# A hybrid encoder block on one core: the last projection with tokens on the output rows

## The chip, the core and the metric
The kernel runs on one core of one Trainium2 chip. Its time is the device time of one execution, in microseconds (us). The engines are PE (TensorE, matrix products into PSUM), DVE (VectorE), ACT (ScalarE), POOL (GpSimd) and SP (SyncE, which here issues most DMAs). They run beside each other, each in the order in which its instructions were written down, and wait for each other by semaphores.

## What is computed
One encoder layer on 512 tokens of width 2048, in float32: a projection into two recurrent mixers (gated DeltaNet and RWKV-7), an output projection, cross attention into 256 memory tokens, an MLP and a final norm.

```python
xn = _rmsnorm(h, norm_mix[l])
y = xn @ w_in[l]
...
h = h + mixed @ w_out[l]
h = h + _cross_attention(_rmsnorm(h, norm_xattn[l]), _rmsnorm(mem, norm_mem[l]), ...)
hn = _rmsnorm(h, norm_mlp[l])
h = h + jnp.square(jax.nn.relu(hn @ mlp_w_up[l])) @ mlp_w_down[l]
return _rmsnorm(h, norm_final)
```
`mlp_w_up` is 2048 x 8192 and `mlp_w_down` 8192 x 2048. "Up" and "down" below are these two products.

## The kernel before
The residual stands with features on partitions: `hres` is 16 tiles of 128 features x 512 tokens, and `hp` are the same tiles as 8 pairs. Weights are the stationary operand, and tokens move.

Precision: each float32 operand is cut into two float32r parts, `hi` (a cast on ACT) and `lo` (the rest, a subtraction on DVE). A product is hi·hi + hi·lo + lo·hi, three matmuls.

Order: up and down, like the mixers, are written as generators ("chains", lines 1737 to 2115). A list scheduler, `run`, takes at each step the instruction that can start first by its own table of costs (`cost`, `start`), where a chain's rank delays it by 150 ns a step, so the order on each engine, SP's queue among them, is fixed when the program is built. The first part of the program (mixers, key projection `kp`, key-query product `kq`) is one such schedule, and up with down another.

Up: 32 units `("u", p, 0)`, each a 2x2 block product by seven products instead of eight (Strassen-Winograd: B11, B21, B22, T1 to T4). The weight sums s1 to s4 that these need are made by DVE in `adds`; `splits` cuts the weights; `multiply_` issues 8 steps per product, one matmul of 512 columns (hi and lo of 256 token columns side by side) and one of 256. `upout` collects, `squared_` applies the squared ReLU and stores the result to DRAM (`Ud`), and `differences` makes the block sums of half of the units and stores them too (`Xd`).

Down, `units` from line 1730 on, by groups of 1024 hidden rows:
- Groups 0 to 6 have four units each, one for each 512 output columns. The first unit (in group 0 the first two) is plain, `"p"`: four weight tiles of 128 output features, 8 steps of three matmuls with all 512 tokens moving. The others are `"d"`: seven products with 256 columns moving, 24 matmuls each, their weight sums made by `adds` as in up.
- Group 7 is a loop of its own behind the scheduler (line 2176): 32 half tiles of plain products, and in between it the sums of squares of the final norm, by a matmul with ones.
- `plainadd` and `downout` add the banks to `hres` and `hp`; `norm_` has multiplied these by the root of the MLP's norm before, one pair in every fourth up unit.
- `abloads`, `direct_` and `crossed` bring the activations back from DRAM and cut them; group e's blocks are freed by its last unit.
- Buffers: 6 raw weight tiles of 128 x 1024 (`wfree`), 3 cut ones (`hfree`), 8 PSUM banks under five tags.

The end: the second half's sum of squares, a square root and a reciprocal on two columns, a matmul that spreads the result over rows, 16 multiplications and 16 stores.

Of the kernel before, what the change touches and what calls it, by code (L numbers as in the profile page):

```python
# [17 lines left out]
P = 128  # L18
# [55 lines left out]
def build(tc, I, out):  # L74
# [106 lines left out]

    def where(a):
        n = a.tensor.name
        k = slot.get(n, n)
        assert holder.get(k, n) == n, (n, holder[k])
        return k
# [92 lines left out]
    def run():  # L279


        while chains:
            best = None
            for c in list(chains):
# [19 lines left out]
                key = (t + (0 if c[3][0][0] == "PE" else 150 * c[1]), c[1])  # L304
# [71 lines left out]
    kpo = [(0, 0), (1, 0), (0, 1), (1, 1)] + [(n, h) for n in range(2, KD) for h in range(2)]  # L376
    hk = [("w", I["wk"][n][:, h * 1024:(h + 1) * 1024]) for n, h in kpo]
# [151 lines left out]
    def projections():  # L529
# [509 lines left out]
    def gdn(h):  # L1039
# [99 lines left out]
        yield from inverse_levels(f"gi{h}", Tm, Tt, N3, ("gkn", "gk", "gqn"), TtG)  # L1139
        vns, Ss = tl("gE"), tl("gEG")  # L1140
# [74 lines left out]

    issue(pieceload(0))
# [8 lines left out]
    for k in range(6, XA):  # L1225
        issue(xload(k))
    chain(pieces(), 1)
# [455 lines left out]
    Ud = [pd.tile([P, 2, 512], F32, name=f"ud{i}", tag=f"ud{i}") for i in range(32)]  # L1683
    pu_cm = tc.tile_pool(name="pu", bufs=1, reuse_waits="tile")
    pu = pu_cm.__enter__()
    Xd = [pd.tile([P, 1024], F32, name=f"xd{i}", tag=f"xd{i}") for i in range(28)]
    uhl = [], []
# [11 lines left out]
    SV = Lane(nc.scalar, "ACT")  # L1699

# [4 lines left out]
    sfree, abfree = buffers(2, "ws"), buffers(2, "ab")  # L1705
# [29 lines left out]
    A11, A21, A22, A12 = range(4)  # L1735

    def loads():
        for u in units:
            kind, e, g = u
            if kind == "p":  # L1740
                todo = [(n, I["w_dn"][e, g * 4 + n]) for n in range(4)]
            else:
                src = I["w_up"][e] if kind == "u" else I["w_dm"][e, g]
                todo = [(i, src[i]) for i in ((A11, A12, A22, A21) if u == units[0] else (A11, A21, A22, A12))]
            for i, src in todo:
                raws[u, i] = r = yield from take(wfree)
                yield SY.dma_start(r, src)
                events.add(("raw", u, i))
        yield lambda: ("raw", units[-1], A12) in events
        r = yield from take(wfree)  # L1750
        raws["last"] = r
        yield SY.dma_start(r, I["w_dn"][7, 0])
        events.add(("raw", "last"))
# [19 lines left out]
    def adds():  # L1773
        for u in units:
            if u[0] == "p":
                continue
# [23 lines left out]
    def splits():  # L1800
        for u in units:
            if u[0] == "p":
                for n in range(4):
                    yield after("raw", u, n)
                    halves[u, n] = hl = yield from take(hfree)
                    yield from cut(raws[u, n], *hl)
                    wfree.append(raws[u, n])
                    events.add(("cut", u, n))
                continue
# [14 lines left out]
        yield after("raw", "last")  # L1824
        yield lambda: any(x is lastpair[0] for x in hfree)
        hfree[:] = [x for x in hfree if x is not lastpair[0]]
        yield from cut(raws["last"], *lastpair[0])

    lastpair = [hfree[-1]]

# [3 lines left out]
    def multiply_():  # L1834
        for u in units:
            kind, e, g = u
            if kind == "p":
                yield lambda: all(("dir", e, k) in events for k in range(4))
                for n in range(4):
                    pt, key = yield from bank("mm", f"dn{e}_{g}_{n}")  # L1840
                    yield after("cut", u, n)
                    hi, lo = halves[u, n]
                    for k in range(8):
                        sl = slice(k * P, k * P + P)
                        uh, ul = direct[e, k]
                        yield mmr(pt, hi[:, sl], uh, k == 0)
                        yield mmr(pt, hi[:, sl], ul)
                        yield mmr(pt, lo[:, sl], uh, stop=k == 7)
                    hfree.append(halves[u, n])
                    chain(plainadd(e, 4 * g + n, pt, key), 1)  # L1850
                continue
            first = u == units[0]
            for i, w in order_of(u):
# [9 lines left out]
                if kind == "u":  # L1863
                    for zs in (range(7), range(7, 8)) if first else (range(8),):
                        for k in zs:
                            yield mmr(pt, hi[:, k * P:k * P + P], comb[i][k], fresh and k == 0)
                        for k in zs:
                            yield mmr(pt[:, HA], lo[:, k * P:k * P + P], comb[i][k][:, HA], stop=k == 7)
                    if e == 31:
                        tfree.extend(comb[i])  # L1870
                else:
                    yield lambda: all(i in blocks.get((e, k), ()) for k in range(4))
                    for q in range(2):
                        o = pt[:, q * M:q * M + M]
                        for k in range(4):
# [451 lines left out]
```

## Time and profile before
| | us |
|---|---|
| three runs, median (lowest to highest) | 2946.62 (2946.21 to 2946.89) |
| the profiled execution, its own time | 2946.95 |
| its span | 2945.2 |

A profile comes from one execution. Its page gives the busy time of each engine, the span in 40 slices, the chain of work that ended last, and groups of equal instructions. A group's line names the source line, the engine, the operation and output<-inputs; then come busy time, mean ns of one, and the idle time before it with what ended that. Most instructions of the scheduled parts have line L251, where the scheduler issues them, so groups are told apart by tile names: `py` is the input projection, `kq` the key-query product, `mxu`, `mmu` and `mgu` are up's banks, `dn` a plain unit's, `mxd`, `mmd` and `mgd` those of the seven-product units. Matmuls are pipelined, so the distance from one start to the next tells more than a duration. In a timeline the first number is the start, the second the length.

### The profile page before, as it was taken

Reading aid. Unit: us, or ns where it says so; the run is one execution under the profiler, and the core shown is the slowest. Engines: PE = TensorE matmul, PEld = TensorE weight load, DVE = VectorE, ACT = ScalarE, POOL = GpSimd, SP = SyncE. Lnnn points to the kernel's source line nnn. Section 1 sums busy time; section 2 is a strip of 40 time slices with the busy share of each in tenths; the row PEclk is TensorE's granted clock in tenths of the full one; section 3 lists DMA queues with packets and bytes.
Section 4 is the critical chain, followed back from the end, with each engine's and each line's share of the span. In section 5 each row is a group of like instructions: output and inputs, shape, how many; then the busy total and the mean of one; then the engine's idle time right before and its main releaser. Section 6 shows DMA issues by size and latency. Waiting matters only on the chain.

```text
span 2945.2 us, 51704 instructions
## 1 busy us (share of the span) xinstructions
PE 2920.6 (99%) x20570; PEld 2527.8 (86%) x20570; DVE 2317.8 (79%) x3535; ACT 1552.3 (53%) x2227; POOL 213.9 (7%) x552
## 2 busy tenths in 40 slices
PE   9999999999999999999999999999999999999998
PEld 7877787887778888889988888888888999999997
DVE  7677676676778767679848998989898888888877
ACT  7455555555556655654436555555555444444434
POOL 0212302302223000000000000000000000000000
PEclk9999999999999999999999999999999999999999
DMA  5323332332425487774323344444445534444435
GB/s 188 113 86 86 98 97 82 98 97 82 132 75 174 167 281 250 253 239 135 109 86 101 136 150 148 146 147 154 144 158 186 186 141 147 150 166 150 143 113 181
DMA packets 228451, 425.22 MB, mean 144 GB/s; under 512 B 92073, under 2 KB 115885, under 8 KB 228209
## 3 DMA queue, kind: packets, MB, share of 16 engines
q1 hardware_dynamic: 211216, 388.35, 40.3%
q10 hardware_dynamic: 16992, 33.56, 3.0%
q8 instruction: 162, 2.65, 0.4%
q14 instruction: 81, 0.66, 0.1%
HBM read 366.91 MB, written 54.93 MB: 143 GB/s over the span
## 4 chain that ended last, share of the span: by engine, by line
PE 95%; DMA 2%; DVE 1%; ACT 1%; issue 0%; ACTq 0%; SPq 0%; DVEq 0%
PE py L251 23%; PE mxu L251 12%; PE mxd L251 8%; PE mgu L251 6%; PE dn L251 6%; PE op L122 5%; PE mgd L251 4%; PE kp L251 3%; PE vp L122 3%; PE dn L122 3%; PE sc L122 3%; PE at L122 3%; PE mmu L251 3%; PE kq L251 2%; PE mmd L251 2%; DMA wraw<-in_wo 1%
## 5 line engine op out<-in xcount | busy, mean ns | idle before, releaser
L251 ACT CAST whi<-wraw 128x1024 fp32r<-128x1024 f32 (+1 forms) x328 | 342.9, 1047 | 357.7 <-PE py L251 159.4
L251 DVE TENSOR_TENSOR wlo<-wraw,whi 128x1024 fp32r<-128x1024 f32 (+1 forms) x328 | 401.2, 1225 | 107.8 <-ACT whi L251 102.8
L251 PE MATMUL py<-xhi,whi 128*128 128x512 f32 x928 | 374.1, 403 | 7.0 <-ACT xhi L251 7.0
L251 PE MATMUL py<-xhi,wlo 128*128 128x512 f32 x928 | 374.2, 403 | 0.0
L251 PE MATMUL py<-xlo,whi 128*128 128x512 f32 x928 | 374.1, 403 | 0.0
L251 PE MATMUL mxu<-cb,whi 128*128 128x512 f32 x1016 | 255.4, 393 | 0.0
L251 ACT CAST whi<-w 128x1024 fp32r<-128x1024 f32 x145 | 151.8, 1051 | 155.1 <-PE mxd L251 36.9
L251 PE MATMUL mxd<-cb,whi 128*128 128x256 f32 x1280 | 233.3, 284 | 0.0
L131 DVE TENSOR_TENSOR wlo<-wraw,whi 128x1024 fp32r<-128x1024 f32 x143 | 174.7, 1223 | 46.9 <-ACT whi L130 45.8
L251 PEld LDWEIGHTS mxu<-cb,whi 128*128 128x128 f32 x1016 | 183.1, 189 | 33.0 <-ACT sl L251 0.2
L251 PEld LDWEIGHTS py<-xhi,whi 128*128 128x128 f32 x928 | 175.4, 189 | 41.4 <-ACT xhi L251 7.0
L251 PEld LDWEIGHTS py<-xlo,whi 128*128 128x128 f32 x928 | 175.4, 189 | 36.0 <-issue 2.5
L251 PEld LDWEIGHTS py<-xhi,wlo 128*128 128x128 f32 x928 | 175.3, 189 | 34.6 <-issue 1.0
L251 PEld LDWEIGHTS mxd<-cb,whi 128*128 128x128 f32 x1280 | 200.3, 192 | 0.5
L130 ACT CAST whi<-wraw 128x1024 fp32r<-128x1024 f32 x143 | 149.8, 1048 | 88.6 <-PE op L122 29.0
L251 DVE TENSOR_TENSOR wlo<-w,whi 128x1024 fp32r<-128x1024 f32 x145 | 176.8, 1222 | 17.3 <-ACT whi L251 17.3
L251 PE MATMUL mxd<-cb,wlo 128*128 128x256 f32 x640 | 181.5, 284 | 0.0
L251 ACT CAST whi<-ws 128x1024 fp32r<-128x1024 f32 x104 | 109.4, 1052 | 124.6 <-PE mxd L251 60.0
L251 PE MATMUL dn<-cb,whi 128*128 128x512 f32 x512 | 158.1, 390 | 0.0
L2218 POOL TENSOR_TENSOR h<-h,rstd 128x256 f32<-128x256 f32 x5 | 3.5, 722 | 1993.0 <-ACT rstd L2212 1993.0
L251 PEld LDWEIGHTS mxu<-cb,wlo 128*128 128x128 f32 x1016 | 138.9, 191 | 9.9
L251 PE MATMUL mxu<-cb,wlo 128*128 128x256 f32 x1016 | 142.2, 283 | 0.0
(913 smaller groups left out, 7214.0 us busy)
## 6 DMA issues: line engine op xcount, KB each, us to landing
wraw<-in_w_in SPq DMA_DIRECT2D x116, 512.0 KB, 3.6
wraw<-in_w_up SPq DMA_DIRECT2D x65, 512.0 KB, 3.5
w<-in_w_up SPq DMA_DIRECT2D x63, 512.0 KB, 3.7
wraw<-in_w_dn SPq DMA_DIRECT2D x48, 512.0 KB, 3.5
ab<-ud SPq DMA_DIRECT2D x46, 512.0 KB, 4.5
w<-in_w_dm SPq DMA_DIRECT2D x41, 512.0 KB, 3.5
wraw<-in_w_dm SPq DMA_DIRECT2D x39, 512.0 KB, 3.7
wraw<-in_wk SPq DMA_DIRECT2D x32, 512.0 KB, 3.9
```

The source lines that it names most:

```text
L122: PE.matmul(o, l, r, start=start, stop=stop, skip_group_check=again)
L130: S.copy(hi, src)
L131: V.tensor_tensor(out=lo, in0=src, in1=hi.bitcast(F32), op=ALU.subtract)
L251: f(*a, **k)
L2218: GP.tensor_tensor(out=h, in0=h, in1=rstd[:, HB], op=ALU.mult)
```

## The change
Down is turned round: the cut activations are the stationary operand and the weights move, 512 output columns at a time, into banks of 128 tokens x 512 features. All eight groups of rows are done by seven products: four groups `e` of 2048 hidden rows by two halves `m` of the output, 8 units; each product has four weight pieces `x` of 128 x 1024, and each piece 12 matmuls.

The weight sums s1 to s4 of all of down don't depend on the input tokens, and are made ahead, in pieces, by chains of their own with a high rank: four loads from DRAM, four DVE operations, four stores to DRAM (`Sd`), all issued by SP. The built program makes 57 pieces of 410 columns in the first schedule (until `kp` ends), then 9 during up and 10 during down, of up to 512 columns. Down then loads sums like any weights.

The residual is turned to token-major in 16 groups of four PE transposes during up, ACT scaling each by the MLP norm's column as it leaves PSUM. The final norm's sum of squares is then a sum along the row: ACT squares with an accumulating output, DVE multiplies by the gain (a new input, the gain repeated over partitions), and one root per token tile scales the rows. The output is stored as rows.

Smaller: product B21 of up's even units takes the hi and lo parts of its activations into the same 256 columns (`narrow`), which takes one DVE addition away; block sums of activations are stored for group 0 alone and made in down for the others; the first `kq` product waits for the last inverse of the mixers; the last norm's column of squares in up is four matmuls with one column each.

```diff
+    def presum(e, m, c, n, d, Q=None):
...
+        a11, a21, a22, a12 = b = [x[:, 0:n - c] for x in d]
+        for i in (A21, A22, A11, A12):
+            yield Q.dma_start(b[i], src[i][:, c:n])
+        for j, op in (("s1", tt(a22, a21, a22, ALU.add)), ("s3", tt(a21, a11, a21)),
+                      ("s2", tt(a11, a22, a11)), ("s4", tt(a12, a12, a11))):
+            yield op
+            yield Q.dma_start(Sd[e, m, j][:, c:n], op[5])
...
+            if i == 0:
+                yield after("inverted", 7)
             yield after("kp", KD - 2 + i) if i < 2 else after("kq", i - 2)
...
+    def ahead():
+        yield after("rows")
+        for j in range(NSET):
+            chain(presums([tl(f"ds{j}{i}", PIECE, shape=[P, PIECE]) for i in range(4)], PIECE, after("kp", 15)),
+                  lambda eng: 2 if eng == "SP" else PRANK)
...
-    units = [("u", p, 0) for p in range(32)]
-    for e in range(7):
-        units += [("p" if g < 1 + (e == 0) else "d", e, g) for g in range(4)]
+    units = [("u", p, 0) for p in range(32)] + [("d", e, m) for e in range(4) for m in range(2)]
...
+                    for x in range(4):
+                        yield after("half", u, i, x)
+                        yield after("block", e, i, x)
+                        hi, lo = halves[u, i, x]
+                        bh, bl = blocks[e, i, x]
...
+                            for part, w_ in enumerate((hi, lo)):
+                                for t in ts:
+                                    o = banks_of[u, tag[0], t][0]
+                                    for kk in range(2):
+                                        c, d = slice(kk * M + t * P, kk * M + t * P + P), slice(kk * 512, kk * 512 + 512)
+                                        yield mmr(o, bh[:, c], w_[:, d], fresh and x + part + kk == 0, stop=x == 3 and part + kk == 2)
+                                        if part == 0:
+                                            yield mmr(o, bl[:, c], w_[:, d])
...
+                        if narrow(e, i):
+                            for part in (HA, HB):
+                                yield mmr(pt[:, HA], w_, comb[i][k][:, part], fresh and k + part.start == 0)
...
-        for i in range(8):
-            yield after("mul", units[4*i+3], B11)
-            yield tt(hp[i], hp[i], rstd.unsqueeze(1).broadcast_to([P, 2, T]), ALU.mult)
...
+                    yield [TE.transpose(pt[:, j * P:j * P + P], hres[4 * g + j][:, t * P:t * P + P], ident)
+                           for j in range(4)]
+                    chain(turned_(g, t, pt, key, free.pop(0)), 0.5)
...
+    def block(e, i, j, ab):
+        blocks[e, i, j] = h, l = yield from own(2)
+        yield from cuts((ab, h, l))
+        events.add(("block", e, i, j))
...
+    def final(t, g):
+        h = H[t, g]
+        c = yield from take(cfree)
+        yield AC.activation(c, h, AF.Square, accum_out=cols5[t][:, g:g + 1])
+        cfree.append(c)
+        yield after("wf")
+        yield tt(h, h, wf[g // 2][:, g % 2 * 512:g % 2 * 512 + 512], ALU.mult)
...
+    def store(t):
+        a, b = rows5[t][:, 0:1], rows5[t][:, 1:2]
+        yield DV.tensor_reduce(out=a, in_=cols5[t], axis=AX.X, op=ALU.add)
+        yield AC.activation(b, a, AF.Sqrt, scale=1.0 / 2048)
+        yield DV.reciprocal(out=b, in_=b)
...
+    def remaining():
+        left = [(e, m, c, min(c + 512, 2048)) for e, m in todo for c in range(upto.get((e, m, "s4"), 0), 2048, 512)]
+        yield after("xd", 7)
+        chain(leftover(left, abfree, lambda d: True, after("ud", 26, 1)), lambda eng: 4)
...
-    for s in range(32):
-        if s:
-            collect(s - 1)
-        if s < 31:
-            wts[s + 1] = wload(I["w_dn"][7, where_[s + 1][0]])
...
```
The loop behind the scheduler, with its own sums, is gone.

More of the change, by code (lines that the diff above doesn't have):

```diff
@@ L1226, in build @@
         issue(xload(k))
+    chain(ahead(), 3)
     chain(pieces(), 1)
@@ L1885, in multiply_ @@
                 if i == B11:
[L1886 removed]
+                    chain(upout(u), 0.2)
             if first:
                 pt, key = yield from bank("scg", "pss2")
[L1889 to L1890 removed]
+                for t in range(4):
+                    yield TE.matmul(pt[:, t:t + 1], acc[:, t * P:t * P + P], ones[:, 0:1], start=True, stop=True)
+                chain(norm_(pt, key), -1)
     banks_of, direct, blocks = {}, {}, {}
@@ L1896, in grab, with gains, narrow @@
         yield tt(o, pt[:, HA], o)
-    def gains(o, pt):
-        for part in (HA, HB):
+    def gains(o, pt, parts=2):
+        for part in (HA, HB)[:parts]:
             yield tt(o, o, pt[:, part])
+    def narrow(p, i):
+        return i == B21 and p % 2 == 0
     def squared_(p, j, c):
@@ L1940, in upout @@
             y, ky = banks_of[u, "mm"]
-            yield from gains(c1[:, HA], y)
+            yield from gains(c1[:, HA], y, 2 - narrow(p, B21))
             events.add(ky)
@@ L1966, in upout @@
         y, ky = banks_of[u, "mm"]
-        yield from gains(c1[:, HA], y)
+        yield from gains(c1[:, HA], y, 2 - narrow(p, B21))
         events.add(ky)
@@ L2115, in build, with turnover @@
     chain(activations(), 1.2)
+    chain(finals(), 1)
+    def turnover():
+        yield after("cut", units[31], "s4")
+        yield lambda: len(sfree) == 2
+        abfree.extend(w[:, i * T:i * T + T] for w in sfree for i in range(2))
+    chain(turnover(), 1)
+    chain(remaining(), lambda eng: 4)
     run()
     manual.__exit__(None, None, None)
-    order = tc.manual_schedule(engines={nc.vector.engine, nc.scalar.engine})
-    order.__enter__()
-    acc = ph.tile([P, T], F32, tag="acc", name="acc3", bufs=1)
```

489 lines of the change are left out of this document (225 added, 264 removed).

## The prediction, made before the change was run
> **What bounds the kernel now.** I read the page first, then the busy time by stretch, then the order of time inside the stretches that change.
>
> ```profile
> span 2945.2 us, 51704 instructions
> PE 2920.6 (99%) x20570; PEld 2527.8 (86%) x20570; DVE 2317.8 (79%) x3535; ACT 1552.3 (53%) x2227; POOL 213.9 (7%) x552
> PE 95%; DMA 2%; DVE 1%; ACT 1%; issue 0%; ACTq 0%; SPq 0%; DVEq 0%
> ```
> PE is busy from end to end, and the chain that ended last is 95% PE. A busy PE may still hide short gaps, so the test is the pace from start to start, below.
>
> ```profile
> core 0: us, PE busy (x) PEld busy (x) DVE busy (x) ACT busy (x) POOL busy (x), PEclk, DMA share, GB/s
> 0.00:1020.00 1020.00, 1012.03 (x8909) 817.12 (x8910) 721.41 (x1325) 572.85 (x816) 210.40 (x547) 1.00 0.37 111
> 1020.00:1110.00 90.00, 89.91 (x511) 78.19 (x511) 61.18 (x98) 53.85 (x97) 0.00 (x0) 1.00 0.84 271
> 1630.00:2259.60 629.60, 627.61 (x3588) 551.51 (x3587) 566.68 (x755) 354.23 (x491) 0.00 (x0) 1.00 0.43 151
> 2259.60:2929.00 669.40, 668.24 (x4635) 624.82 (x4635) 575.12 (x743) 293.52 (x382) 0.00 (x0) 1.00 0.45 157
> ```
> The rows are the front (mixers, input projection), the key-query stage, up, and down. The granted clock is 1.00 in each. DVE has 299 us free in the front; up and down run it at 90% and 86%.
>
> ```profile
> L251 PE MATMUL mxd<-cb,whi x1280: 278/284/284, 2303.3 to 2837.0; 128*128 128x256 f32 x183
> L251 PE MATMUL mxu<-cb,whi x1016: 386/394/793, 1630.3 to 2258.5; 128*128 128x512 f32 x170
> L251 PE MATMUL dn<-cb,whi x512: 388/390/492, 2259.7 to 2776.3; 128*128 128x512 f32 x171
> L251 PE MATMUL kq<-khl,whi x256: 388/398/500, 1019.6 to 1109.9; 128*128 128x512 f32 x128
> ...
> 2399.98 0.40 PE L251 MATMUL mgd<-cb,whi 128*128 128x256 f32 x2
> 2400.22 0.28 PE L251 MATMUL mgd<-cb,wlo 128*128 128x256 f32 x1
> 2400.34 0.40 PE L251 MATMUL mgd<-cb,whi 128*128 128x256 f32 x2
> ```
> The first four lines are per tile (min/median/max ns, first to last start). Down opens with two plain units, 192 matmuls of 512 columns, from 2259.7 to 2303.3: 43.6/192 = 0.227 us each. In the seven-product units three matmuls of 256 columns take 0.36 us, 0.120 each. So 512 columns cost less than twice 256: each 256-column matmul pays 0.0065 us beside its columns.
>
> **The change part by part.**
>
> *Down.* Before: 768 plain matmuls of 512 columns, 20 units x 7 x 24 = 3360 of 256, and for the last group 256 of each, so 1024 wide and 3616 narrow. 1024 x 0.227 + 3616 x 0.120 = 666.3 us. The trace has 671.6 (2259.7 to the first matmul after down at 2931.29, below); 5.3 us are waits. After: 8 units x 7 products x 4 weight pieces x 12 = 2688 matmuls, all of 512 columns (the built order has this number): 610.2 us, and the same share of waits, 4.9, makes 615.1. The term is -56.5. Bounds: no waits, 0.2267 a piece, 609; or the pace of up,
>
> ```profile
> 2240.10 2.00 PE L251 MATMUL mxu<-cb,whi 128*128 128x512 f32 x8
> 2241.94 1.12 PE L251 MATMUL mxu<-cb,wlo 128*128 128x256 f32 x8
> ```
> 1.84/8 = 0.230, with 4.9 of waits 623. I take 615: the plain units are the nearest row, with a new stationary tile for each 512 columns, as in the new order.
>
> "TensorE: Matmul & The Clock Gate" of the Trainium skill, section "Back-to-back issue gap", gives N/2.4 + 2.5 ns for a warm matmul, 215.8 ns for 512 columns and 109.2 for 256. By it the old down would be 615.9 and the new 580.1, an estimate of -36, so it speaks for a smaller gain. The measured 0.227 and 0.120 decide here.
>
> *What feeds down.* 224 weight pieces are cut (8 units x 28), one each 12 x 0.227 = 2.72 us of PE.
>
> ```profile
> L251 DVE TENSOR_TENSOR wlo<-wraw,whi 128x1024 fp32r<-128x1024 f32 (+1 forms) x328 | 401.2, 1225 | 107.8 <-ACT whi L251 102.8 <-DMA E<-bg16U 3.3 <-DMA gE<-Rd 0.4
> L251 ACT CAST whi<-wraw 128x1024 fp32r<-128x1024 f32 (+1 forms) x328 | 342.9, 1047 | 357.7 <-PE py L251 159.4 <-PE mxd L251 38.7 <-PE mgd L251 29.3
> L251 DVE TENSOR_TENSOR cb<-ab,cb 128x512 fp32r<-128x512 f32 (+1 forms) x128 | 71.9, 595 | 8.7 <-ACT cb L251 8.4
> L251 ACT CAST cb<-ab 128x512 fp32r<-128x512 f32 (+1 forms) x128 | 65.2, 544 | 68.3 <-DMA ab<-ud 47.5 <-DMA ab<-xd 16.9 <-DVE ab L251 2.9
> L251 DVE TENSOR_TENSOR h<-h,mxd 128x512 f32<-128x512 f32 x80 | 54.8, 686 | 20.1 <-PE mxd L251 19.2
> L251 DVE TENSOR_TENSOR r<-r,sr 128x512 f32<-128x512 f32 x15 | 10.3, 690 | 0.8
> L251 DVE TENSOR_TENSOR sl<-sl,mmu 128x256 f32<-128x256 f32 x64 | 26.8, 419 | 7.6 <-PE mmu L251 6.5
> ```
> DVE: 224 x 1.225 + 112 output adds x 0.686 + 112 block cuts x 0.595 + 104 sums and gains x 0.69 = 490 us in 615, 80% against 86%; ACT 224 x 1.05 and 112 x 0.54. Neither binds. A bank is added 10.9 us (48 matmuls) before its next product, so no PE wait there. DMA: 224 x 0.524 MB, 10 leftover sum pieces of 2.1 MB and 20 MB of activations make 158 MB, 257 GB/s; the key-query row moves 271 and keeps PE at 89.91 of 90. At the seam the first blocks need tiles that the last up unit frees with its first product, six products (some 17 us) ahead, against 4 x (0.54 + 0.6). Cost nothing; without that cover the wait would be some 5 us, once.
>
> *Up.* In 16 units product B21 takes the hi and lo parts of its activations one after the other, 256 narrow matmuls for 128 wide ones: 128 x (0.240 - 0.227) = +1.7. The 64 transposes of the residual are new PE work:
>
> ```profile
> 73.19 0.60 PE L251 MATMUL prt<-cst,gE 128*128 128x128 f32 x4
> 73.55 0.48 PE L251 MATMUL py<-xhi,whi 128*128 128x512 f32 x1
> 73.86 0.39 PE L251 MATMUL py<-xlo,whi 128*128 128x512 f32 x1
> ```
> Four take 0.36, and the next matmul 0.31 where it should take 0.227: 0.44, times 16, +7.1. DVE loses 8 scalings of 1.22, 24 differences and 16 adds of 0.42 (26 us) and gains 36 leftover sums of 0.69 (25 us): as full as before. The column sum of squares (2 matmuls for 4 tiny ones) is even.
>
> *The front.* 57 pieces of sums: 228 DVE ops of 410 columns, 0.58 us each (0.69 less 102 columns at 0.53/512, from 1.22 and 0.69), 133 us in 299 us of idle time: DVE rises from 71% to 84%. SP issues 456 more DMAs (the last input-projection load stands at place 759 instead of 369 of its queue) at a third of a us, and a store that waits for its sum holds the loads behind it. What says that there is room:
>
> ```profile
> 2905.41 0.34 SPq L151 DMA_DIRECT2D wraw<-in_w_dn  x1
> ACT whi L251 <- PE py L251: 159.4, 77, 6.2
> DVE y L251 <- PE py L251: 47.8, 50, 3.6
> sl<-in_xT SPq DMA_DIRECT2D x16, 256.0 KB, 2.6
> gE<-Rd SPq DMA_DIRECT2D x8, 256.0 KB, 5.2
> L251 POOL TENSOR_TENSOR sr<-sr,sr 64x15 f32<-64x15 f32 (+7 forms) x120 | 45.0, 375 | 9.4
> ```
> The weight cuts wait for PE to free buffers, not PE for cuts. With 96 MB more the front moves some 205 GB/s. Up, with DVE at 90%, takes 629.4 us for 1792 x 0.347 = 621.8 of matmuls, 1.2% of waits; the same share of the front would be 12 us. The floor is 0 (PE loses none of its work, so no gain), the ceiling the rival below. I take 5. The hold on the key-query product for the last inverse costs nothing: in the built order that inverse's matmuls end 110 places before it anyway.
>
> *Tail.*
> ```profile
> 2931.29 0.28 PE L122 MATMUL pss<-cst,acc 128*128 128x1 f32 x2
> 2935.86 4.40 DVE L2220 SCALAR_TENSOR_TENSOR h<-h,prm,row 128x256 f32<-128x256 f32 x11 [1.83 <-ACT rstd L2212]
> 2936.37 6.15 ACTq L2222 DMA_DIRECT2D out_dram<-h  x8
> 2936.65 5.14 SPq L2222 DMA_DIRECT2D out_dram<-h  x8
> ```
> From 2931.3 to 2945.2 it is 13.9 us, 2.7 of it after the last issue. After: result 0.3, two adds, squares, sums, root and scalings of two token tiles on DVE and ACT some 5, the last issue 0.4, 2.7: 8.5 (7 to 10). Term -5.4.
>
> *Sum.* 2945.2 - 56.5 + 1.7 + 7.1 + 5 - 5.4 = 2897.1 of span. The profiled execution took 2946.95, 1.75 more than its span, and stood 0.33 above the median 2946.62, so 2898.5; I say 2898.
>
> **The rivals.**
> 1. *The front's sums starve PE* (slower). DVE runs in order, so a sum whose four loads are late holds every mixer op behind it, and PE then waits in its own order. Against 2.6 us landing in quiet time there are 5.2 us behind other transfers: 2.6 late x 57 pieces = 148 us in place of 5, 3041. It outweighs the rest from 0.93 us a piece on (53/57). For it: 1640-byte rows, and transfers in two directions. Against: DVE's remaining 166 us of idle time, and the cuts' lead.
> 2. *GpSimd is locked out.* The mixers' inverses run on POOL, 210 us in the front, beside sums that read two tiles each; if all sums that fall on POOL work stop it, 133 x 0.206 = 27 us, and all reach PE: 2920. For it: POOL sits on a chain of small DMAs; against: POOL's ops keep a mean of 0.375 us beside a DVE that is 71% busy, much of it with two such operands already. The rule is in "SBUF — State Buffer" of the Trainium skill, "SBUF: two separate sides": a DVE op with two SBUF inputs and a GpSimd op exclude each other for a whole instruction.
> 3. *Down becomes bound by DMA.* Were 250 GB/s the most that it gets, 158 MB take 632 us instead of 615: 2915. For: loads and sums share SP's queue; against: the 271 row.
> 4. *The wide pace isn't held.* At 0.240 the 2688 take 645 + 5: 2933. For: up's 0.230 lies on that side of 0.227; against: it is only a quarter of the way.
>
> That the change doesn't do what it says is excluded by the built order's counts.
>
> **How the numbers follow.** Forecast 68% (own range 2885 to 2914: down 609 to 623, front 0 to 12, tail 7 to 10), rival 2 10%, rival 3 7%, rival 4 6%, rival 1 9%. The range 2884 to 2934 takes in all but rival 1 and the forecast's edges. What a measurement of this kernel can tell from no change is about 0.2%, 6 us: faster is everything but rival 1, less a little of its mild end, 0.90; same 0.02; slower 0.08.
>
> **What would show it.** Right: down from first to last matmul 609 to 623 us; `mxd` starts 0.227 apart; up longer by 7 to 11; the key-query product starting within 12 us of 1019.6; a tail of 7 to 10. Wrong: a front over 1035; DVE waiting on the sums' loads; POOL ops far over 0.375 us; ACT's casts in down waiting for weight loads; a pace of 0.235 or more.

## The result and the profile after

The changed kernel takes 2956.65 us (median of 9 runs, 2949.85 to 2962.97) against 2945.04 us before (9 runs on the same chip, 2942.09 to 2946.89): a ratio of 1.004, 95% interval 1.0028 to 1.0051. It is slower by some 12 us, where 48 us less were forecast. The profiled execution took 2957.76 us with a span of 2955.7; the granted clock is 0.994 where it was 0.998.

Busy time by stretch in the changed kernel (front, up, down; columns as in the prediction):

```profile
0.00:1083.00 1083.00, 1031.50 (x8900) 827.00 (x8901) 832.17 (x1546) 567.03 (x809) 231.97 (x547) 0.99 0.67 191
...
1696.00:2334.00 638.00, 635.91 (x3784) 565.06 (x3783) 564.90 (x744) 362.36 (x508) 0.00 (x0) 1.00 0.54 173
2334.00:2942.00 608.00, 608.00 (x2684) 503.20 (x2684) 462.95 (x553) 304.62 (x367) 0.00 (x0) 1.00 0.77 256
```

And its matmuls by tile (min/median/max ns, first to last start):

```profile
L256 PE MATMUL kq<-khl,whi x256: 387/396/504, 1083.7 to 1176.9; 128*128 128x512 f32 x128
...
L256 PE MATMUL mxu<-cb,whi x1016: 387/393/478, 1696.2 to 2333.1; 128*128 128x512 f32 x170
...
L256 PE MATMUL mxd<-whi,cb x512: 389/389/499, 2334.3 to 2866.6; 128*128 128x512 f32 x171
```

The first starts cut the execution at the same places as before. The key-query product starts at 1083.7 us instead of 1019.6: the front lost 64.1. From there to up it is 612.5 against 610.7 (+1.8), up takes 638.1 against 629.4 (+8.7). Down runs with PE busy 608.00 of 608.00 us.

The order of time at the end:

```profile
2943.42 0.61 PE L256 MATMUL scgd<-wlo,cb 128*128 128x512 f32 x2
...
2945.55 0.69 DVE L256 TENSOR_TENSOR h<-h,ab 128x512 f32<-128x512 f32 x1
...
2949.50 1.81 SPq L256 DMA_DIRECT2D out_dram<-h  x3
```

The last matmul ends at 2944.0: down took 609.7 instead of 671.6 (-61.9). The tail is 11.7 instead of 13.9 (-2.2). 64.1 + 1.8 + 8.7 - 61.9 - 2.2 = 10.5, the difference of the two spans. What down gained is lost in the front. There PE did the same work (8900 instructions with records, 8909 before) with 51.5 us of idle time instead of 8, and was busy some 19 us longer at a clock of 0.99.

What the front waits for. Waits of its engines (us, times, longest; the second line is that of the kernel before), then of SP's queue (0 to 1080 us), then DMA issues (KB each, median us from issue to landing; the last line is again that of the kernel before):

```profile
POOL sgj L256 <- DMA sgi<-ndgi: 216.1, 8, 34.6
...
POOL sgj L251 <- DMA sgi<-ndgi: 138.5, 8, 28.7
...
DVE ds L256 <- DMA ds<-in_w_dm: 92.8, 34, 6.9
```
```profile
SPq L256 <- DVE ds L256: 155.3, 152, 5.0
SPq L256 <- DMA sd_s<-ds: 108.9, 68, 4.0
```
```profile
ds<-in_w_dm SPq DMA_DIRECT2D x184, 205.0 KB, 4.1
sd_s<-ds SPq DMA_DIRECT2D x184, 205.0 KB, 4.3
...
E<-bg16U SPq DMA_DIRECT2D x32, 64.0 KB, 5.4
ndri<-GA SPq DMA_DIRECT2D x8, 128.0 KB, 5.1
ndri<-GB SPq DMA_DIRECT2D x8, 128.0 KB, 5.4
...
ndri<-GB SPq DMA_DIRECT2D x8, 128.0 KB, 2.6
```

DVE stood 92.8 us in 34 places in front of a sum whose loads had not landed. SP stood 109 us in front of loads whose tile was still being stored, and 155 us in front of stores whose sum was not made. GpSimd's wait for the bounce through `ndgi` rose from 138.5 to 216.1. And several of the mixers' own transfers land later: `ndri<-GB` took 2.6 us before and takes 5.4, `E<-bg16U` 2.5 and 5.4, `ndgi<-gEs` 3.4 and 4.0. Not all do: `sr<-ndri` took 6.3 before and takes 2.7. Every order here is fixed when the kernel is built, and the planner that writes it out lets a transfer land 2.9 us after its issue, later only where the bytes before it, counted at 300 GB/s, are not through:

```
t, eng = max(state["dma"] + 700, t + 2900) + slack[1], "DMA"
```

So there are several candidates: late loads in front of DVE, the traffic itself, the issues in SP's queue, the DVE ops, GpSimd shut out by them. The yardstick of all runs below is the first start of the key-query product. Single profiles of one front differ: two kernels with the same front (`x4_late_model`, `x14_two_sets`) had it at 1038.0 and 1043.4, so differences under some 6 us are not read. Every version also has an order of its own, which the planner writes anew; how far that alone moves the front was not measured. Where no other number of runs is given, a version was run once.

### The profile page after: what moved, and what is told of

It is laid out like the page before. It is cut to its first block, busy times and chain, and to the rows that moved or that the text cites. A ratio compares the mean times of both kernels' runs of the same rounds, so it can differ in the third digit from the quotient of the medians.

```text
span 2955.7 us, 49493 instructions
## 1 busy us (share of the span) xinstructions
PE 2886.4 (98%) x18794; PEld 2428.0 (82%) x18794; DVE 2317.0 (78%) x3559; ACT 1573.5 (53%) x2233; POOL 232.0 (8%) x547
## 5 line engine op out<-in xcount | busy, mean ns | idle before, releaser
L256 ACT CAST whi<-wraw 128x1024 fp32r<-128x1024 f32 (+1 forms) x374 | 392.0, 1049 | 423.1 <-PE py L256 147.4
L256 DVE TENSOR_TENSOR wlo<-wraw,whi 128x1024 fp32r<-128x1024 f32 (+1 forms) x374 | 459.3, 1229 | 113.9 <-ACT whi L256 104.1
L256 ACT CAST whi<-w 128x1024 fp32r<-128x1024 f32 x190 | 200.1, 1054 | 222.7 <-PE mxu L256 47.4
L256 DVE TENSOR_TENSOR wlo<-w,whi 128x1024 fp32r<-128x1024 f32 x190 | 231.7, 1221 | 64.2 <-ACT whi L256 63.7
L256 DVE TENSOR_TENSOR ds<-ds,ds 128x410 f32<-128x410 f32 (+1 forms) x228 | 134.3, 589 | 99.7 <-DMA ds<-in_w_dm 95.4
L131 DVE TENSOR_TENSOR wlo<-wraw,whi 128x1024 fp32r<-128x1024 f32 x112 | 136.7, 1222 | 45.1 <-ACT whi L130 44.0
L256 PEld LDWEIGHTS mxu<-cb,wlo 128*128 128x128 f32 x1016 | 138.7, 190 | 10.5 <-DVE wlo L256 0.7
L256 PE MATMUL mgu<-cb,whi 128*128 128x512 f32 x512 | 129.4, 394 | 1.8 <-ACT whi L256 1.8
L256 PE MATMUL mxd<-whi,cb 128*128 128x512 f32 x512 | 126.8, 389 | 0.0
L256 PE MATMUL mgd<-whi,cb 128*128 128x512 f32 x512 | 126.4, 389 | 0.0
L122 PE MATMUL op<-ob,whi 128*128 128x256 f32 (+1 forms) x752 | 115.3, 304 | 0.3 <-ACT whi L130 0.3
```

The source lines that it names most:

```text
L122: PE.matmul(o, l, r, start=start, stop=stop, skip_group_check=again)
L131: V.tensor_tensor(out=lo, in0=src, in1=hi.bitcast(F32), op=ALU.subtract)
L256: f(*a, **k)
```

## The experiments

### The parts of the sums, one by one

`x1_no_front_sums`: no sums ahead, plain blocks in their place.
```
-        for j in range(NSET):
-            chain(presums([tl(f"ds{j}{i}", ...
...
+                    if isinstance(w, str) and (f, m) in unsummed:
+                        w = A21
```


> The 57 pieces of weight sums are left out of the front (loads, DVE ops and stores); the products of down that would read them read a plain weight block instead, so the output is not the reference's. Up, down, the 19 leftover pieces and the tail are those of the changed kernel. Theory A (late loads: a sum whose loads have not landed holds DVE in order), theory B (traffic: the sums' loads and stores slow the small transfers of the mixers themselves) and theory C (the ops: the time of the 228 DVE ops, or their shutting out of GpSimd) all put the 64 us on the sums, so all expect the key-query product to start at 1019 to 1023 us as before (1019.6) and a time of 2957 - 64 = 2893 us. If the front stays over 1060, it is none of them but the hold on the key-query product or the changed order.

`x3_front_dve_only`: the ops on tiles that stay in place.
```
+        for n in range(57):
+            for op in (tt(a22, a21, a22, ALU.add), tt(a21, a11, a21), tt(a11, a22, a11), tt(a12, a12, a11)):
+                yield op
```


> The 228 DVE ops of the 57 pieces run on four tiles that stay in place, with no loads and no stores; down reads plain blocks for these sums, so the output is not the reference's. Theory A: nothing is late, the key-query product starts at 1020 to 1032, time 2893 to 2905. Theory B: as A. Theory C: the ops alone cost it, it starts at 1060 to 1085, time 2935 to 2957, with GpSimd's mean op well over 375 ns if it is the lock.

`x2_front_dma_only`: the transfers without the ops.
```
-            yield op
+            if ops:
+                yield op
             yield Q.dma_start(Sd[e, m, j][:, c:n], op[5])
```


> The 57 pieces are loaded and stored as in the changed kernel, but without their DVE ops: the four loaded tiles are stored as they are, so the output is not the reference's. Theory A: no DVE op waits for these loads, the key-query product starts at 1020 to 1030, time 2893 to 2903. Theory B: the same bytes and rows move, it starts at 1060 to 1085, time 2935 to 2957. Theory C: 1020 to 1025, time 2893 to 2898.

`x4_late_model`: the planner lets the sums' loads land 5.0 us later.
```
+    SM5 = Lane(nc.sync, "SP", margin=5000.0)
...
-            yield Q.dma_start(b[i], src[i][:, c:n])
+            yield (Q or SM5).dma_start(b[i], src[i][:, c:n])
```


> The scheduler is told that each load of the front's sums lands 5.0 us later than it assumed (7.9 us after its issue in place of 2.9), so that each sum takes a later place in DVE's order; 41 pieces are made ahead in place of 57, the other sums in up and down. The same result. Theory A: DVE no longer waits for the loads, under 20 us in all in place of 95; the key-query product starts at 1022 to 1040, up and down lose some 5 us to 19 more leftover pieces: time 2897 to 2920. Theory B: 41/57 of the traffic, 41/57 x 64 = 46 us, it starts at 1066, time 2940. Theory C: as B, 1066 and 2940.

The key-query product in the first, without sums:

```profile
L256 PE MATMUL kq<-khl,whi x256: 389/397/403, 1021.0 to 1110.8; 128*128 128x512 f32 x128
```

The same in the second, the ops alone, and its largest group on GpSimd (busy us, mean ns | idle before):

```profile
L256 PE MATMUL kq<-khl,whi x256: 389/396/499, 1032.7 to 1123.6; 128*128 128x512 f32 x128
```
```profile
L256 POOL TENSOR_TENSOR sr<-sr,sr 64x15 f32<-64x15 f32 (+7 forms) x120 | 60.2, 501 | 9.4
```
The same in the third, the DMA alone, and what SP's queue waited for in its front (us, times, longest):

```profile
L256 PE MATMUL kq<-khl,whi x256: 389/396/403, 1116.2 to 1206.4; 128*128 128x512 f32 x128
```
```profile
SPq L256 <- DMA sd_s<-ds: 127.6, 72, 4.9
SPq L256 <- DMA ds<-in_w_dm: 102.7, 86, 4.5
```
And in the fourth, placed late, with DVE's sums (busy us, mean ns | idle before) and PE's longest wait:

```profile
L256 PE MATMUL kq<-khl,whi x256: 387/396/501, 1038.0 to 1127.8; 128*128 128x512 f32 x128
```
```profile
L256 DVE TENSOR_TENSOR ds<-ds,ds 128x410 f32<-128x410 f32 (+1 forms) x164 | 95.6, 583 | 3.1
```
```profile
PE mxd L256 <- ACT whi L256: 62.1, 1, 62.1
```

Times: 2894.5, 2902.5, 2987.0 and 2973.9 us. Without the sums the front is back (1021.0, and 2894.5 against the 2893 expected): all of the loss is theirs, and the new hold on the key-query product costs nothing. The ops alone cost 11.7 us (1032.7), at the edge of theory A and well short of C, although GpSimd's ops do get longer beside dense DVE ops (501 ns in this group, 375 before). The DMA alone missed every expectation: 95 us, more than the whole change. With no op between, SP itself stands 230 us in its queue, in front of stores whose load has not landed and of loads whose tile is not yet stored, and what is queued behind it is the mixers' transfers. The pieces are also packed closer: they move between 73 and 667 us, with 236 GB/s from 150 to 600 us, where the changed kernel spreads them up to 1095 us, with 186. Late placement brought the front to 1038.0 as theory A said, with DVE's wait for its loads down from 99.7 us to 3.1; but 41 pieces are not 57, and the total missed: the sums left for down were late for its last unit, one wait of 62.1 us.

### Placing all 57 later, one DMA a piece, and GpSimd

> The same result, and all 57 pieces made ahead as in the changed kernel, the same loads and stores; only the scheduler is told, as in the run with 41 pieces, that the sums' loads land 5.0 us later than it assumed, and their rank among DVE's work is raised from 4 to 2 so that 57 fit. Theory A (late loads held by in-order waits): DVE waits under 20 us for these loads, the key-query product starts at 1033 to 1048 us (1032.7 with the ops alone), up (638) and down (609.5) stay as in the changed kernel, time 2907 to 2922. Theory B (the traffic itself): it starts at 1075 to 1085, time 2949 to 2958.

> The same result and 57 pieces, but the four loads of a piece are one DMA and its four stores one: 114 issues on SP in place of 456, the same bytes and the same 1640-byte rows; the load is taken to land 5.0 us later, rank 1. Theory A: as the run before it, the key-query product at 1033 to 1048, time 2907 to 2922; if SP's issues and waits are a part of the loss, this one is the faster by some us. Theory B: 1075 to 1085, time 2949 to 2958.

> The same result; no sums in the front, all 64 pieces of 512 columns in up (30) and down (34), on GpSimd, which has no other work there. A 512-column op of GpSimd took 1.35 us in the front, so 256 ops are 346 us in 1250. If DVE and GpSimd do not hold each other up: front 1021, up 638 to 645, down 610 plus a wait for the last sums of 0 to 60 us: time 2895 to 2960. If they exclude each other (rival 2 of the prediction), the DVE ops of up, 90% busy, are longer than 1.23 us a cut and up takes over 660: time over 2930 without any wait in down.

> The same result; 25 pieces ahead in the front with the late-landing assumption (on DVE), 30 in up and the other 14 in down on GpSimd. Theory A: front 1025 to 1035, no wait for sums in down. Without mutual exclusion up is 638 to 645 and the time 2898 to 2912; with it up is over 660 and the time over 2925. Theory B: 25/57 x 64 = 28 us in the front, 1049.

The edits, the first two with the late landing of `x4_late_model` kept: in the first the rank, and 57 pieces; in the second the four loads of a piece as one and its four stores as one, at rank 1; in the last two the engine of the sums that are left, which may also start earlier in down.
```
-    NSET, PIECE, PRANK = 1, 410, 4
+    NSET, PIECE, PRANK = 1, 410, 2
...
+        yield LL.dma_start(d, I["w_dm"][e, m][:, :, c:n].rearrange("a p c -> p a c"))
...
-                yield from presum(*left.pop(0), r, SY)
+                yield from presum(*left.pop(0), r, SY, GS)
```

Measured 3010.7, 3029.4, 3079.2 and 2951.6 us. The first two are plain misses: the key-query product at 1136.8 and 1154.8, later than with the change as it was. For the first, the product and one stretch of the front (columns as above; the last but two is the granted clock):

```profile
L256 PE MATMUL kq<-khl,whi x256: 387/396/504, 1136.8 to 1230.5; 128*128 128x512 f32 x128
```
```profile
600.00:700.00 100.00, 82.11 (x746) 65.15 (x745) 72.38 (x144) 39.83 (x60) 25.85 (x67) 0.88 0.63 184
```

DVE hardly waits for the sums' loads any more (9.8 us), so theory A as worded, with DVE's waits as the whole cause, falls. The traffic theory gives no more than 1085. Something in the order itself had to cost; `x15_rank2` below returns to it.

The GpSimd runs left the front alone (1020.8 with no piece, 1027.0 with 25 pieces placed late, as theory A expected, not 1049 as B) and lost 54 us in up (692 us); the one with no piece ahead then waited 113 us more in down for sums that were late. Groups of `x8_pool_some_ahead` in up:

```profile
L256 POOL TENSOR_TENSOR ab<-ab,ab 128x512 f32<-128x512 f32 x90 | 173.7, 1929 | 1044.6 <-DMA ab<-in_w_dm 1039.9
...
L256 DVE TENSOR_TENSOR wlo<-wraw,whi 128x1024 fp32r<-128x1024 f32 x81 | 112.6, 1391 | 11.0 <-ACT whi L256 9.9 <-DMA ab<-ud 0.5 <-DMA w<-in_w_up 0.5
```

The cuts take 1391 ns in place of 1220, and GpSimd's op 1929 in place of the 1353 that one of the same size took in the front before; the shortest of these 90 took 1265 ns, the median 2152. "SBUF — State Buffer" of the Trainium skill, section "SBUF: two separate sides", says that a DVE op with two SBUF inputs and a GpSimd op that reads SBUF hold the shared port pair one after the other, each for its whole instruction; the direction agrees, the size is these rows. Up, with DVE 90% busy, cannot bear it. Down with 14 pieces on GpSimd could: from the first to the last `mxd` start it is 532 us in the changed kernel and 534 here.

### Transfers without waits, and with the ops beside them

> The loads and stores of the 57 pieces without their DVE ops, as in the run with the DMA alone (the loaded tiles are stored as they are, so the output is not the reference's), but each of them is put into SP's queue 4 us later than the scheduler thinks that it could go, so that SP hardly waits for a landing. Theory H (in-order queues, DVE's and SP's, held by transfers that have not landed; the bytes themselves cost little): SP's waits for the sums' loads and stores fall from 230 us to under 40, the key-query product starts at 1021 to 1035 us, time 2893 to 2908. Theory B (the traffic itself): the same 96 MB before the same stage, it starts at 1065 to 1085, time 2938 to 2958.

> The same result. 53 pieces ahead (rank 3): loads taken to land 3.0 us later, a load put 2.0 us after the modelled landing of the store that frees its tile, a store 1.5 us after the modelled end of its sum; the rest of the sums (12 pieces in place of 10) in down may start one unit earlier. Theory H: DVE and SP both wait little, the key-query product starts at 1033 to 1050 (12 of that are the DVE ops), up and down as in the changed kernel, time 2907 to 2924. Theory B: 53/57 of the loss or more, 1079 to 1100, time 2953 to 2975.

> The DMA of the run before last (57 pieces, no waits for it) and, unconnected with it, as much DVE time as the sums take: 350 ops of 205 columns on a tile that stays in place. The output is not the reference's. Theory H: the two add, the key-query product starts at 1033 to 1048, time 2905 to 2921. Theory B: over 1075, time over 2948. If it is DVE's ops and the transfers together that cost it (a port that both use, with no wait in between), the DMA alone is at 1021 to 1035 and this one over 1060.

The first two lines are in `x9_dma_no_wait` and `x11_dma_and_dve_apart`, the last two in the latter alone:
```
+    LD = Lane(nc.sync, "SP", wait=4000.0)
+    ST = Lane(nc.sync, "SP", wait=4000.0)
...
+        for n in range(350):
+            yield DV.tensor_tensor(out=x, in0=x, in1=x, op=ALU.subtract)
```

Products of the first and the third:

```profile
L256 PE MATMUL kq<-khl,whi x256: 389/396/497, 1045.4 to 1136.1; 128*128 128x512 f32 x128
```
```profile
L256 PE MATMUL kq<-khl,whi x256: 387/396/486, 1060.9 to 1154.6; 128*128 128x512 f32 x128
```

2916.6, 3007.6 and 2934.1 us. All three lie outside both theories' bounds. The case of a port that both use, named for the last, fails by its first half: the DMA alone is at 1045.4, not 1021 to 1035. With slack the transfers alone cost 24.4 us over `x1_no_front_sums`, not 95. SP's waits for them are 65 us, not 230, but the slack also spreads them, up to 1014 us, so waits and packing together made most of the loss of `x2_front_dma_only`, and their shares are not shown. The mean rate alone does not tell the loss: from 150 to 600 us this version moves 194 GB/s and PE is busy 446.9 of 450 us, while the changed kernel moves 186 and PE is busy 431.2.

Ops and transfers unconnected cost 39.9, close to 11.7 + 24.4. The changed kernel costs 62.7. That leaves some 23 us to what `x11_dma_and_dve_apart` lacks, the connection: a sum that waits for its load, a store that waits for its sum, a load that waits for the store. It is a difference of two versions, not a part that was measured. `x10_slack` (rank 3) lost 110 and fits neither theory.

### What of the transfers costs, and a version that could win

> The front's 456 loads and stores alone, without DVE ops and with 4 us of slack in SP's queue as in the run with the DMA that waits little (the key-query product at 1045.4), but 51 columns of each piece in place of 410: an eighth of the bytes, the same number of DMAs and of rows; down reads plain blocks for these sums, so the output is not the reference's. Theory B' (of the 24 us that these DMAs cost, the bytes are the cause: they make other transfers land later): the key-query product starts at 1021 to 1028, time 2892 to 2900. Theory Q (SP's queue is the cause: 456 more issues and their waits delay the issue of the mixers' transfers): 1040 to 1047, time 2911 to 2918.

> The same again with all the bytes, but one DMA for the four loads of a piece and one for its four stores: 114 issues in place of 456 (output not the reference's: no DVE ops, the loaded blocks are stored as they are). Theory B': the bytes stay, 1040 to 1050, time 2911 to 2921. Theory Q: 1021 to 1030, time 2892 to 2901.

> The same result. 41 pieces ahead with the late-landing assumption as in the first such run (key-query product at 1038.0), and in down a second set of four tiles, free there already, so that the other sums are no longer late for the last unit (62 us of one wait there). The wait gone: 1038 front, up 638, down 610 to 616, time 2912 to 2920, about 1% faster than before. If the second set only adds traffic to down (326 GB/s at most), weight loads come late and down is over 630: time over 2933.

```
-            yield Q.dma_start(b[i], src[i][:, c:n])
+            yield LQ.dma_start(b[i], src[i][:, c:n]) if Q else LQ.dma_start(b[i][:, 0:51], src[i][:, c:c + 51])
...
+        second = pair + [hp[7][:, 0], hp[7][:, 1]]
+        yield from leftover(left, second, lambda d: True)
```

The products of the first two, with few bytes and with few DMAs:

```profile
L256 PE MATMUL kq<-khl,whi x256: 389/396/403, 1023.9 to 1114.1; 128*128 128x512 f32 x128
```
```profile
L256 PE MATMUL kq<-khl,whi x256: 387/396/504, 1032.9 to 1124.8; 128*128 128x512 f32 x128
```

The same 456 DMAs with an eighth of the bytes cost 2.9 us (2896.3 us in all), less than is read here; all the bytes in a quarter of the DMAs (56 pieces) cost 11.9 (2905.5 us), all the bytes in all the DMAs 24.4. So the issues alone are nearly free and the bytes are needed for a loss, as theory B' said of the first; but in the second its 1040 to 1050 and the other's 1021 to 1030 are both missed: the number of DMAs counts once the bytes are there. `x14_two_sets` took 2928.05 us (4 runs), ratio 0.9942, interval 0.9925 to 0.9959: the wait of 62 us is gone, down grew by 14 and the front stands at 1043.4, so it is 8 us over its expectation and 0.6% faster than before.

### Rank and landing time, one at a time

> As the version with two sets (41 pieces, key-query product at 1043.4 us there), but the sums' rank among DVE's work is 2 in place of 4, so that they go ahead of the mixers' steps (ranks 3 and 4) where both could start; capped at the same 41 pieces. The same result. If the rank is what made the run with 57 late pieces so slow (1136.8), the key-query product starts at 1070 to 1110, time 2955 to 2995. If it was the number of pieces, it starts at 1035 to 1050, time 2920 to 2936.

> The same result. The changed kernel with two sets in down, and one assumption of the scheduler changed for the whole front: every transfer, the mixers' own too, is taken to land 5.0 us after its issue in place of 2.9 (measured medians there: 2.6 to 5.4); 47 pieces ahead, rank 4. If planning with late landings is what recovers the loss, the key-query product starts at 1030 to 1048 with 47 pieces, time 2908 to 2930. If the transfers themselves set it, 47/57 of 64, it starts at 1074, time 2954.

> The same result. One DMA for the loads and one for the stores of a piece, 38 pieces ahead at rank 4, all landings in the front taken as 4.2 us (the sums' loads 1.5 us more, and 0.5 to 1 us of slack ahead of their issue), two sets in down. The quarter of the issues was worth 12 us with DMA alone: the key-query product starts at 1026 to 1038, time 2903 to 2918. If down with 27 pieces left gets short of transfers, it is over 625 and the time over 2920.

The edit of the second, with the two sets in down the whole of it:
```
-            t, eng = max(state["dma"] + 700, t + 2900) + slack[1], "DMA"
+            t, eng = max(state["dma"] + 700, t + state.get("lat", 2900)) + slack[1], "DMA"
...
+    state["lat"] = 5000
     issue(pieceload(0))
...
-    state.update(table="e", dma=0.0, shape=None)
+    state.update(table="e", dma=0.0, shape=None, lat=2900)
```

The product of `x14_two_sets`, with rank 4, and that with rank 2; then that of `x16_late_all` with its first 1000 us; then the same stretch of the changed kernel:

```profile
L256 PE MATMUL kq<-khl,whi x256: 389/396/501, 1043.4 to 1134.6; 128*128 128x512 f32 x128
```
```profile
L256 PE MATMUL kq<-khl,whi x256: 389/396/478, 1100.2 to 1192.8; 128*128 128x512 f32 x128
```
```profile
L256 PE MATMUL kq<-khl,whi x256: 389/396/403, 1032.7 to 1124.6; 128*128 128x512 f32 x128
```
```profile
0.00:1000.00 1000.00, 983.08 (x8624) 793.38 (x8628) 794.40 (x1454) 551.12 (x787) 234.25 (x547) 0.99 0.64 185
```
```profile
0.00:1000.00 1000.00, 953.27 (x8316) 760.02 (x8317) 766.52 (x1424) 527.14 (x751) 226.98 (x537) 0.99 0.67 190
```

Rank 2 alone moved the product from 1043.4 to 1100.2 (2984.6 us), as expected if the rank was at fault: sums that go ahead of the mixers' steps wherever both could start make those late, and everything behind them. Such sums are also done sooner, by 701 us in place of 1071, but denser traffic alone is not it: from 300 to 450 us this version moves 186 GB/s and the changed kernel 185, and PE is busy 136.9 of 150 us in the one and 145.5 in the other. The loss over `x1_no_front_sums` is 1.9 us a piece here and 2.0 in `x5_late_57`, so rank 2 accounts for that miss. For `x6_one_dma` at rank 1 and `x10_slack` at rank 3 it is the likely cause, not tried alone.

`x16_late_all` settles most of the rest. It moves 185 GB/s through the first 1000 us, against 190 in the changed kernel, makes 47 pieces ahead on DVE, and PE is busy 983 us against 953. Its product starts at 1032.7, 11.7 us after that of `x1_no_front_sums`, which the ops alone cost for 57 pieces. DVE waits 12.3 us for the sums' loads. It took 2916.17 us (4 runs, 2913.03 to 2919.78), ratio 0.9903, interval 0.9888 to 0.9918: 1% faster than before, the fastest of the versions that leave nothing out, and within its expectation. One number of the planner, 2.9 us that should have been nearer 5, with the extra set in down for the 10 pieces less, turns the loss into a gain. One lucky order is not the reason: all five versions that plan later at rank 4 (`x4_late_model`, `x8_pool_some_ahead`, `x14_two_sets`, `x16_late_all` and `x17_one_dma_late_all`, with 25 to 47 pieces) have the product between 1027.0 and 1043.4.

What later planning takes away is DVE's waiting, not SP's. SP's two waits for the sums in `x16_late_all` (0 to 1080 us):

```profile
SPq L256 <- DVE ds L256: 132.7, 119, 4.3
SPq L256 <- DMA sd_s<-ds: 75.4, 50, 4.7
```

That is 208 us, 4.4 a piece, against 264 us and 4.6 a piece in the changed kernel, while DVE's wait for loads fell from 1.6 us a piece (92.8/57) to 0.3 (12.3/47). So SP's waits by themselves do not set the loss.

`x17_one_dma_late_all` had the earliest front of these (1029.7, as expected) and took 2940.48 us (10 runs; ratio 0.9985, interval 0.9976 to 0.9995), 0.15% faster than before: with more sums left to down (650 us there) it has the other ending that its expectation names. PE's wait in it, and down's fullest stretch in `x16_late_all`:

```profile
PE mxd L256 <- ACT whi L256: 22.4, 1, 22.4
```
```profile
2584.00:2660.00 76.00, 75.26 (x329) 61.10 (x328) 58.48 (x72) 31.58 (x34) 0.00 (x0) 1.00 0.97 337
```

## Why the prediction was wrong, point by point

*The step that failed is the front's term.* It said: "The floor is 0 (PE loses none of its work, so no gain), the ceiling the rival below. I take 5." It measured 64.1. The term was worked out from one thing, how full DVE gets, and priced by up, where a DVE at 90% loses 1.2%. That part held: the ops alone cost 11.7 us (`x3_front_dve_only`), within its 0 to 12. What had no price was the transfers: 24 us by themselves even with slack, and some 23 more where sums, loads and stores hang on each other. The prediction counted them ("SP issues 456 more DMAs", "some 205 GB/s") and gave them no term. It had a row for bandwidth, the key-query stage that keeps PE full at 271 GB/s, and used it for down, where it held. For the front such a row would have been no answer. The front's mixers pass their inverses through DRAM in short steps, each planned to land after 2.9 us; in the changed kernel the medians of `ndri` are 5.1 and 5.4, that of `E` is 5.4, and the sums' own loads take 4.1. The room was one of bandwidth; what ran out was the lead that the plan allowed for a landing, as `x16_late_all` shows, which moves nearly the same traffic with a longer lead.

*Rival 1* had the mechanism in part, at 9%. Its ingredient was near: 5.2 us for a late landing, 4.1 to 5.4 measured. Its price was not: 148 us, for 57 pieces each fully late on PE's path. DVE met 34 late loads, 92.8 us in all, and the front lost 64.1/57 = 1.12 us a piece, just over its own 0.93 from which it outweighs the gains. It looked at DVE alone, and that was the better half: SP's queue is held longer (264 us), but `x16_late_all` holds it 208 us with the front nearly back. It did not see that the mixers' own transfers are late too. So the change ends near the point of decision, the mild end of rival 1, for which only a part of its 9% was left.

*Rival 2* (GpSimd locked out) isn't what made the loss: the group that stood at 375 ns is at 386 in the changed kernel, and all of GpSimd's work in the front went from 210 to 232 us. The effect exists where ops are dense: in `x3_front_dve_only` this work took 257 us, more than in the changed kernel, and the front lost 11.7 us in all. *Rival 3* put the limit of down at 250 GB/s; PE ran 608.00 of 608.00 us at 256. No sharp limit shows above it either: of the four fullest stretches of 76 us of down in `x16_late_all`, PE is full in one, at 335 GB/s, and loses 6.2 us in the other three, at 308, 317 and 337. *Rival 4* is out: 609.7/2688 = 0.2268 a matmul.

*Down*: right, and a little more than taken: -61.9 against -56.5, at the lower bound (609), since the waits that were carried over (4.9) are not there. *Up*: +8.7 against +8.8; its two parts were not measured apart. *The hold* on the key-query product: nothing, as said (1021.0 with it and without the sums). *The tail*: the term was mis-sized, -2.2 against -5.4. From the last matmul's end it takes 7.3 us to the end of the last issue, where 5.7 were allowed, and 4.4 behind that, where 2.7 were.

With the front's term right, the same sum gives 2945.2 - 56.5 + 8.8 + 64.1 - 5.4 = 2956.2, against the 2955.7 of the span. That it comes so near is in part luck: down is 5.4 us better than its term, the tail 3.2 and the stretch between the key-query product and up, which had no term, 1.8 worse. `x1_no_front_sums`, the forecast without its failed term (2898.5 - 5 = 2893.5), took 2894.5. The range ended at 2934 because it treated the front's ceiling as another case instead of the term's own upper bound.

What stays open: how the 23 us of the connection come about step by step, how much of the gain of `x16_late_all` over `x14_two_sets` (1032.7 against 1043.4) is the mixers' own transfers, and why the number of DMAs costs 12 us only when the bytes are there. SP's waits for these transfers rise with the loss (43, 56 and 65 us for 2.9, 11.9 and 24.4 in `x12_few_bytes`, `x13_quarter_dmas` and `x9_dma_no_wait`), but `x16_late_all` has 208 us of them and loses 11.7 with its ops.

## What to carry to other kernels

Before filling a stage's idle engine time with new transfers, compare what the plan assumes for a landing with what transfers take under the load that will result, for the stage's old transfers too: in a kernel whose queues are ordered at build time, a landing 2 us later than planned can hold all that stands behind it in that order. That one stage carries 256 GB/s with PE full (down) is no evidence for a stage with a chain through DRAM (the front, at 190). And place filler work behind the chain's own steps: rank 2 in place of 4 cost 57 us with the same work.

## What was not expected of the hardware

The same transfer lands at very different times, and the core's mean rate does not tell when. `ndri<-GB` had a median of 2.6 us before, with 111 GB/s in the first 1000 us, and 5.4 in the changed kernel with 190. But in `x17_one_dma_late_all`, with 169, it had 7.3, and in `x16_late_all`, with 185, it stands so:

```profile
ndri<-GB SPq DMA_DIRECT2D x8, 128.0 KB, 2.6
```

What stands about it in the order seems to count more; that was not measured apart. "DMA: Bandwidth & Descriptors" of the Trainium skill, section "Latency and other measured facts", says that the memory's access time grows with load (0.2 us on average, 2 us at high load); the first two numbers agree in direction, the last two do not follow from the load alone.

Where PE waits often, its granted clock is lower too: in the stretch of `x5_late_57` quoted above PE was busy 82 us of 100 and the granted clock stood at 0.88, while it is 1.00 in down of the changed kernel, where PE is full. What the lower clock costs in time was not worked out.

DVE's two-input ops and GpSimd's ops lengthen each other where both run much of the time: by 14% (1220 to 1391 ns) and 43% (1353 to 1929) in up of `x8_pool_some_ahead`.
